# Seven products for a seventh pair of up projections, and GpSimd in place of VectorE for the weight sums

## The chip, the cores and the metric

The program runs on one core of one Trainium2 chip. The metric is the device time of one execution in microseconds; the kernel before has a median of 646.96 us over three runs (646.5 to 647.2). The profile is of one further execution, whose span from the first to the last instruction is 644.9 us; 2.1 us of the median lie outside that span. Engines are named as the profile names them: PE is TensorE, PEld its weight loads, DVE is VectorE, ACT is ScalarE, POOL is GpSimd, SP is SyncE, which issues most DMAs.

## The reference

One decoder layer on 512 tokens of width 1024: attention with a forget gate, a layer norm, a gated MLP with a causal convolution on the gate, a second layer norm, and a gated embedding that is added.

```python
def conv_ffn(x, w_up, conv_w, conv_b, w_down):
    u, g = jnp.split(x @ w_up, [FFN_DIM], axis=-1)
    g = causal_dwconv(g, conv_w, conv_b)
    return (jax.nn.gelu(g, approximate=False) * u) @ w_down
...
x = layer_norm(DEEPNORM_ALPHA * x + mix, ln_mix_g[i], ln_mix_b[i])
ffn = conv_ffn(x, ffn_w_up[i], ffn_conv_w[i], ffn_conv_b[i], ffn_w_down[i])
x = layer_norm(DEEPNORM_ALPHA * x + ffn, ln_ffn_g[i], ln_ffn_b[i])
```

FFN_DIM is 2816, that is 22 blocks of 128 columns, f = 0 to 21. Everything is float32.

## The kernel before, in words

**Products of split numbers.** A float32 product is made of three matmuls: each operand is cut into a high part (`whi`, made by ACT at L123) and the rest (`wlo`, made by DVE at L129 as raw minus high), and `three` (L147, the matmul is L152) adds high x high, high x low and low x high in PSUM.

**Units of weights.** The class `Weights` holds a list of units, up to 128x1024 numbers each, in the order in which PE uses them. SP loads a unit into one of four `raw` buffers (in the MLP every fifth unit goes into a fifth one, a part of the tile `side`). `cut_to` cuts units into `whi` and `wlo`, of which there are five pairs of buffers; in the MLP a unit is cut when PE is four units before it. A unit's cut thus frees the raw buffer for a load four or five units later. A unit may have a `make` function that first forms sums of weight blocks in place.

**Seven products in place of eight.** Some matrix products are done by halves with seven products of blocks in place of eight (a Strassen scheme). The weight side needs sums of blocks: `t12` forms two of them (L207, L208; the block that it subtracts is loaded into a slot of `side` at L204), `t3` one (L215), `t4` one (L222). Each sum is an operation of 128x512. For the down projection, the units of three pairs of blocks at a time (`down`, three parts) are made so. For the up projection, blocks are taken in pairs j = f // 2. Pairs in `UP_PAIRS` use seven products: `up_step` runs four steps for the gate g and for u in turn, three of 24 matmuls of 256 columns and one of 12. The other pairs use plain products of 24 matmuls of 512 columns, two for g and two for u. For pairs in `KEPT` the sums are made early, during attention, and kept in DRAM; the other pairs in `UP_PAIRS` make them with `t12`, `t3` and `t4`.

**Behind a pair.** With seven products the results are gathered in a tile E (L822 and L833 on DVE, L826, L827, L829 and L837 on ACT). After the last step the convolution (L759 on ACT, L760 and L762 on DVE), the GELU (L767, ACT) and the product with u (L768, DVE) run for both blocks at once. Then the operands of the down product are formed: four sums of E (L855 to L858, DVE) and their parts a, b and s (L863 on ACT, L864 on DVE). For a pair in `APART` the earlier pair's operands are formed only inside the first steps of this pair. There is one tile E.

**Order.** From f = 2 on, DVE and ACT keep the order in which the code is written. PE, POOL and SP are put in order by the framework. Units of the down product of the part before are put between the steps of the up product by `CHUNKS`. In pairs 1 and 2 (`DMA_PAIRS`) the low parts of plain units are formed by DMAs with accumulation on POOL's queue (L126); later POOL's queue carries accumulating DMAs that form the sums of the output gate's weights, each behind a small copy that waits for ACT (L279, L280, L281). The adders L659 and L661 add a finished down product to y.

```python
UP_PAIRS = (2, 3, 4, 6, 7, 9)
KEPT = (3, 4, 6, 7)
APART = (2, 3, 4, 7)
RAW_BUFS = 4
SPLIT_BUFS = 5
CHUNKS = (None, (1,) * 12, (1,) * 12, (2, 1) * 4)
```

Of the kernel before, what the change touches and what calls it, by code (L numbers as in the profile page):

```python
# [30 lines left out]

CHUNKS = (None, (1,) * 12, (1,) * 12, (2, 1) * 4)

UP_PAIRS = (2, 3, 4, 6, 7, 9)

KEPT = (3, 4, 6, 7)

DMA_PAIRS = (1, 2)

APART = (2, 3, 4, 7)  # L40
HALF = S // 2
ALPHA = 2.0 ** 0.25
EPS = 1e-5
# [20 lines left out]
class Weights:  # L64
# [40 lines left out]
    def cut_to(self, i):  # L105
        while self.cut < min(i, len(self.units)):
            self.load_to(self.cut + 1)

            self.make(self.cut)
            self.make(self.cut + 1)  # L110
            src, n, inner, make, home, by_dma = self.units[self.cut]
            t = self.raw.pop(self.cut)
            behind = ExitStack()
            if home is not None:
                hi, lo, first = home()
                behind.enter_context(self.tc.issue_after(first))
            else:
                hi, lo = [self.pool.tile([P, UNIT], F32R, tag=g, name=f"{g}{self.cut}", bufs=SPLIT_BUFS)
                          for g in ("whi", "wlo")]
            c = 0  # L120
            for piece in [t[:, :n]] if make is None else self.pieces.pop(self.cut):
                e = c + piece.shape[-1]
                self.nc.scalar.activation(hi[:, c:e], piece, AF.Copy)  # L123
                if by_dma:
                    self.nc.scalar.activation(lo[:, c:e], piece, AF.Copy, scale=-1.0)
                    self.nc.gpsimd.dma_start(lo[:, c:e].rearrange("p (a b) -> p a b", b=inner), src,  # L126
                                             accum_op=ALU.add)
                else:
                    self.nc.vector.tensor_sub(lo[:, c:e], piece, hi[:, c:e].bitcast(F32))  # L129
                c = e  # L130
            behind.close()
            self.parts[self.cut] = (hi, lo)
            self.cut += 1
# [9 lines left out]
def trunk_layer(ctx: ExitStack, tc: tile.TileContext, xT, x2d, pT, wqk, wv0, wv1, wv2, bf, wo, wup, cwb,  # L143
                wdn, wpl, wg, bg, gm, bm, gf, bff, out):
    nc = tc.nc
# [47 lines left out]
    def side(i):  # L193


        return aside[0][:, i, :]

    def t12(b11, i):
        def make(t):
            if t is None:  # L200
                to = side(i)
                if len(b11.shape) == 3:
                    to = to.rearrange("p (a b) -> p a b", b=P)
                nc.sync.dma_start(to, b11)  # L204
                return None
            t1, t2 = t[:, :512], side(i)
            nc.vector.tensor_sub(t1, t1, t2)  # L207
            nc.vector.tensor_sub(t2, t[:, 512:], t1)  # L208
            return [t1, t2]
        return make  # L210

    def t3(t):
        if t is None:
            return None
        nc.vector.tensor_sub(t[:, :512], t[:, 512:], t[:, :512])  # L215
        return [t]

    def t4(i):
        def make(t):
            if t is None:  # L220
                return None
            nc.vector.tensor_sub(t[:, :512], t[:, :512], side(i))  # L222
            return [t[:, :512]]
        return make

# [11 lines left out]
    def up_units(j):  # L237

        f0, f1 = 2 * j, 2 * j + 1
        if j in KEPT:  # L240
            return (lambda q: W.add(wup[f0, 1 - q], inner=P),
                    lambda q: W.add(kept[j, q][:, 0:4:3, :], inner=512),
                    lambda q: W.add([(kept[j, q][:, 2, :], 512), (wup[f1, 1 - q][:, 4:], 512)]),
                    lambda q: W.add(kept[j, q][:, 1, :], n=512))

        def unit(f, q, make=None, k0=0):
            return W.add(wup[f, 1 - q][:, k0:], n=(KD - k0) * P, inner=P, make=make,
                         by_dma=make is None and j in DMA_PAIRS)

        return (lambda q: unit(f0, q), lambda q: unit(f1, q, t12(wup[f0, 1 - q][:, :4], 3 + q)),  # L250
                lambda q: unit(f1, q, t3), lambda q: unit(f0, q, t4(3 + q), 4))
# [33 lines left out]
    for part in range(4):  # L285
# [3 lines left out]
        for i in range(2 * len(fs)):  # L289
            f, q = fs[i // 2], i % 2  # L290
            j, n = f // 2, i % 4
            if j in UP_PAIRS:
                stages = up_units(j)
# [4 lines left out]
            for _ in range(CHUNKS[part][i] if part else 0):  # L298
                if todo:
                    src, c, make = todo.pop(0)  # L300
                    u_dn[part - 1].append(W.add(src, n=c, inner=512, make=make))
            if j in UP_PAIRS and n == 3:
                for sq in range(2):
# [397 lines left out]
    def cut_tiles(kind, n, bufs, name, dtype=F32R, pool=spool):  # L701
        return [pool.tile([P, n, HALF], dtype, tag=f"{kind}{g}", name=f"{name}{g}", bufs=bufs) for g in "hl"]
# [89 lines left out]
    def up_step(j, st, s, E, amid=None):  # L792

        if st == 0:
            ups[j, s] = bank(f"{'gu'[s]}{2 * j}", "two" if j > 2 else None)
        ps = ups[j, s]
        z, x = ps[:, :HALF], ps[:, HALF:]
        hi, lo = W.get(u_up[j, st, s], 4)  # L800
        first, second = slice(0, HALF), slice(HALF, S)

        def go(to, col, on, a=None, sn=None, last=4):
            for k in range(4):
                w = slice((4 * col + k) * P, (4 * col + k + 1) * P)
                if a is None:
                    mh, ml = [v[:, 4 * sn + k, :] for v in xs]
                else:
                    mh, ml = [v[:, a[0] + k, a[1]] for v in (x1h, x1l)]
                three(to, hi[:, w], lo[:, w], mh, ml, k == 0 and not on, k == 3, on=on)  # L810

        e = E[:, (1 - s) * 2 * S:(2 - s) * 2 * S]
        c1 = side(7)[:, s * HALF:(s + 1) * HALF]
        if st == 0:
            go(z, 1, False, a=(4, first))
            go(x, 0, True, a=(0, first))
            nc.scalar.activation(c1, z, AF.Copy)
            nc.scalar.activation(z.rearrange("p (a b) -> p a b", b=P),
                                 zeros.unsqueeze(1).to_broadcast([P, 2, P]), AF.Copy)
            if amid is not None:  # L820
                amid()
            nc.vector.tensor_add(c1 if j in APART else e[:, :HALF], x, c1)  # L822
        elif st == 1:
            go(z, 0, True, sn=0)
            go(x, 1, True, sn=1)
            nc.scalar.activation(e[:, S:S + HALF], x, AF.Copy)  # L826
            nc.scalar.activation(e[:, S + HALF:], z, AF.Copy)  # L827
            if j in APART:
                nc.scalar.activation(e[:, :HALF], c1, AF.Copy)  # L829
        elif st == 2:  # L830
            go(z, 1, True, sn=3)
            go(x, 0, True, sn=2)
            nc.vector.tensor_add(e[:, S:], ps, e[:, S:])  # L833
        else:
            go(x, 0, True, a=(4, second))
            del ups[j, s]
            nc.scalar.activation(e[:, HALF:S], x, AF.Copy)  # L837
# [10 lines left out]
    def operand_sums(E):  # L848


        def e(n):
            return E[:, n * HALF:(n + 1) * HALF]

        a21, a11, a22, a12, s1, s2, s3, s4 = [e(n) for n in range(8)]
        nc.vector.tensor_add(s1, a21, a22)  # L855
        nc.vector.tensor_sub(s2, s1, a11)
        nc.vector.tensor_sub(s3, a11, a21)
        nc.vector.tensor_sub(s4, a12, s2)  # L858

    def operand_parts(ops, E):  # L860
        e3 = E.rearrange("p (a b) -> p a b", b=HALF)
        for (h, l), src in zip(ops, (e3[:, 1:4:2, :], e3[:, 2:3, :], e3[:, 4:, :])):
            nc.scalar.activation(h, src, AF.Copy)  # L863
            nc.vector.tensor_sub(l, src, h.bitcast(F32))  # L864
# [48 lines left out]
    for part in range(4):  # L913
# [3 lines left out]
        def between():  # L917
            for _ in range(next(slots, 0)):
                next(before)

        for f in range(6 * part, min(6 * part + 6, NF)):
# [3 lines left out]
            if f == 2:  # L925

                ordered.enter_context(tc.manual_schedule(
                    engines={mybir.EngineType.DVE, mybir.EngineType.Activation}))
            if q == 0 and j not in APART:
                E = hpool.tile([P, 8 * HALF], F32, tag="E", name=f"E{j}")  # L930
            if f == 0:
# [9 lines left out]
                continue  # L941
            if j in UP_PAIRS:
                if q == 0:
                    up_step(j, 0, 0, E)
                    between()
                    up_step(j, 0, 1, E, (lambda: operand_sums(E)) if j in APART else None)
                    if j in APART:
                        operand_parts(pending.pop(), E)
# [12 lines left out]
            else:  # L961
# [3 lines left out]
                n = 4 * (j - 3 * part) + 2 * q  # L965
# [10 lines left out]
            if q:  # L976
                if part < 3:
                    ops.append([cut_tiles("A", 2, 3, f"a{j}"), cut_tiles("B", 1, 5, f"b{j}", pool=hpool),
                                cut_tiles("S", 4, 4, f"s{j}")])
                    if j + 1 in APART:  # L980
                        pending.append(ops[-1])
# [3 lines left out]
                else:  # L985
# [4 lines left out]
                    ops.append((h, l))  # L990
            if j not in UP_PAIRS:
                between()
# [217 lines left out]
```

## Time and profile before

| | |
|---|---|
| Median of 3 runs | 646.96 us |
| Span of the profiled execution | 644.9 us |
| That execution with what lies outside the span, by the median | 2.1 us more |
| ACT | busy 384.7 us (60%) |
| POOL | busy 125.9 us (20%), 139 instructions |
| DMA, hardware queue of SP | 107.34 MB |

A row of the profile gives the line of the kernel, the engine, the operation, the tile written and the tiles read, the shape, and times. In a timeline the first two numbers are the start and the duration in microseconds; in brackets stands how long the engine was idle before, and for what. In the MLP, pair 0 begins at about 248 us, pair 1 at 271, pair 2 at 293, pairs 3, 4 and 5 at 313, 344 and 376, pairs 6, 7 and 8 at 404, 435 and 467, pairs 9 and 10 at 495 and 532; the last MLP product ends at 566 us.

### The profile page before, as it was taken

The page shows a single profiled execution, that of the slowest core. Times are in us where ns is not written, and L with a number is a line of the kernel's source. Part 1 is how long each engine was busy: PE and PEld are TensorE (multiplying, and loading weights), DVE is VectorE, ACT ScalarE, POOL GpSimd, SP SyncE. Part 2 cuts the span into 40 slices and gives each one's busy share as a digit, 9 for nine tenths or more (in the row PEclk, how much of TensorE's full clock was granted, in tenths as well). Part 3 has the DMA queues.
Part 4 walks back from the last instruction along what each step waited for, and adds up shares of the span by engine and source line. Part 5 has one row for each costly group of instructions (what it writes and reads, how often), then busy time and mean ns, then how long its engine had stood idle before and what let it go on. Part 6 is the DMA issues. An engine that isn't in the chain of part 4 may idle for free.

```text
span 644.9 us, 10078 instructions
## 1 busy us (share of the span) xinstructions
PE 638.9 (99%) x3630; PEld 563.4 (87%) x3630; DVE 533.5 (83%) x870; ACT 384.7 (60%) x685; POOL 125.9 (20%) x139
## 2 busy tenths in 40 slices
PE   8999999999999999999999999999999999999997
PEld 7899888888888889989999988999988998888886
DVE  6764779888888599857889987889897998689997
ACT  6653777877776317946656554647455455336872
POOL 0000544554456043110000010101011001002001
PEclk9999999999999999999999999999999999999999
DMA  8764524444578387684676849765746864681632
GB/s 284 250 236 127 210 85 153 172 177 159 205 256 314 127 261 220 140 219 137 209 219 170 216 132 243 196 212 149 235 130 207 189 219 113 159 283 57 232 113 98
DMA packets 49538, 121.08 MB, mean 188 GB/s; under 512 B 4881, under 2 KB 8721, under 8 KB 49489
## 3 DMA queue, kind: packets, MB, share of 16 engines
q1 hardware_dynamic: 44688, 107.34, 50.6%
q0 software_dynamic: 4800, 13.11, 11.0%
q8 instruction: 28, 0.46, 0.3%
q14 instruction: 22, 0.17, 0.1%
HBM read 107.72 MB, written 18.87 MB: 196 GB/s over the span
## 4 chain that ended last, share of the span: by engine, by line
PE 96%; DVE 2%; DMA 1%; SPq 0%; issue 0%; ACT 0%; DVEq 0%
PE g L152 18%; PE u L152 18%; PE pp L152 14%; PE x L152 8%; PE pl L152 7%; PE pv L152 7%; PE z L152 4%; PE r L152 3%; PE ap L152 3%; PE o L559 3%; PE t L546 2%; PE ao L152 2%; PE y L152 2%; PE s L509 2%; PE s L511 2%; PE p L152 1%
## 5 line engine op out<-in xcount | busy, mean ns | idle before, releaser
L123 ACT ACTIVATE whi<-raw 128x1024 fp32r<-128x1024 f32 (+5 forms) x137 | 128.3, 940 | 92.3 <-issue 12.5
L129 DVE TENSOR_TENSOR wlo<-raw,whi 128x1024 fp32r<-128x1024 f32 (+4 forms) x132 | 140.1, 1069 | 30.3 <-ACT whi L123 29.6
L533 POOL TENSOR_SCALAR pr<-pr,rl 128x128 f32<-128x128 f32 (+1 forms) x64 | 75.5, 1195 | 132.6 <-DVE rl L529 132.6
L280 POOL COPY neghalf<-neghalf 128x1 f32<-128x1 f32 x16 | 10.1, 633 | 246.1 <-ACT neghalf L279 246.1
L152 PE MATMUL g<-x1h,whi 128*128 128x256 f32 (+1 forms) x168 | 54.7, 326 | 0.0
L152 PE MATMUL g<-x1l,whi 128*128 128x256 f32 (+1 forms) x168 | 54.5, 324 | 0.0
L152 PE MATMUL g<-x1h,wlo 128*128 128x256 f32 (+1 forms) x168 | 54.5, 324 | 0.0
L152 PE MATMUL u<-x1l,whi 128*128 128x256 f32 (+1 forms) x160 | 53.0, 331 | 0.0
L152 PE MATMUL u<-x1h,wlo 128*128 128x256 f32 (+1 forms) x160 | 53.0, 331 | 0.0
L152 PE MATMUL u<-x1h,whi 128*128 128x256 f32 (+1 forms) x160 | 53.0, 331 | 0.0
L152 PE MATMUL pp<-xh,wlo 128*128 128x512 f32 x128 | 50.5, 394 | 0.0
L152 PE MATMUL pp<-xl,whi 128*128 128x512 f32 x128 | 50.0, 391 | 0.0
L152 PE MATMUL pp<-xh,whi 128*128 128x512 f32 x128 | 50.0, 391 | 0.0
L525 ACT ACTIVATE pr<-s,nm 128x128 f32<-128x128 f32 (+1 forms) x64 | 33.5, 527 | 9.1 <-DVE nm L521 8.9
L152 PEld LDWEIGHTS g<-x1h,whi 128*128 128x128 f32 x168 | 32.0, 190 | 3.4 <-issue 0.7
L152 PEld LDWEIGHTS g<-x1l,whi 128*128 128x128 f32 x168 | 32.0, 190 | 2.7
L152 PEld LDWEIGHTS g<-x1h,wlo 128*128 128x128 f32 x168 | 32.0, 190 | 2.5
L152 PEld LDWEIGHTS u<-x1h,whi 128*128 128x128 f32 x160 | 30.4, 190 | 3.0
L152 PEld LDWEIGHTS u<-x1l,whi 128*128 128x128 f32 x160 | 30.4, 190 | 2.9
L152 PEld LDWEIGHTS u<-x1h,wlo 128*128 128x128 f32 x160 | 30.4, 190 | 2.8
L123 ACT ACTIVATE whi<-side 128x512 fp32r<-128x512 f32 (+1 forms) x33 | 25.5, 783 | 10.3 <-PE u L152 3.6
L521 DVE CUSTOM_DVE_ANT_0 s<-s,mask 128x128 f32<-128x128 f32 (+1 forms) x64 | 30.0, 510 | 1.7 <-PE s L511 1.5
(635 smaller groups left out, 1869.9 us busy)
## 6 DMA issues: line engine op xcount, KB each, us to landing
raw<-wup SPq DMA_DIRECT2D x34, 512.0 KB, 5.9
raw<-wdn SPq DMA_DIRECT2D x23, 512.0 KB, 4.5
raw<-wqk SPq DMA_DIRECT2D x16, 512.0 KB, 3.3
ka<-wup SPq DMA_DIRECT2D x8, 512.0 KB, 4.2
kb<-wup SPq DMA_DIRECT2D x8, 512.0 KB
kept<-kb SPq DMA_DIRECT2D x8, 512.0 KB, 3.4
kept<-ka SPq DMA_DIRECT2D x8, 512.0 KB, 3.1
raw<-wo SPq DMA_DIRECT2D x8, 512.0 KB, 4.1
```

The costliest lines, as they stand in the source:

```text
L123: self.nc.scalar.activation(hi[:, c:e], piece, AF.Copy)
L129: self.nc.vector.tensor_sub(lo[:, c:e], piece, hi[:, c:e].bitcast(F32))
L152: nc.tensor.matmul(ps, lhsT, rhs, start=start and n == 0, stop=stop and n == 2, skip_group_check=on)
L280: with tc.issue_after(nc.gpsimd.tensor_copy(small[:, m + 32:m + 33], small[:, m:m + 1]).ins):
L509: nc.tensor.matmul(ps[:, :n], QA[:, q], KA[:, :n], start=True, stop=False)
L511: nc.tensor.matmul(ps[:, :n], qb[0:68, q], kb[0:68, :n], start=False, stop=True)
L521: last_mask[:] = [nc.vector.tensor_tensor_reduce(ps[:, :w], ps[:, :w], mask[:, S - w:], -1.0, BIG, op0=ALU.add, op1=ALU.min, accum_out=nm[ ...
L525: nc.scalar.activation(pr[:, off:off + w], ps[:, :w], AF.Exp, bias=nm[:, i:i + 1], scale=-1.0, accum_out=ls[:, i:i + 1])
L533: nc.gpsimd.tensor_scalar_mul(pr[:, off:off + w], pr[:, off:off + w], rl[:, i:i + 1])
L546: nc.tensor.transpose(ps[:, w:w + P], pr[:, o:o + P], ident)
L559: nc.tensor.matmul(ps[:, q0:], V[:, j, h], p[:, o:o + w], start=j == 0 and n == 0, stop=j == NT - 1 and n == 1)
```

## The change

Pair 8 (blocks 16 and 17) joins `UP_PAIRS` and `APART`, so that its up products are seven products of halves; it is not in `KEPT`, so its weight sums are made by `t12`, `t3` and `t4`. All sums of these three functions go from DVE to POOL. `cut_to` calls `make` for the unit that is cut and for the two behind it, where it was for one behind it.

```diff
-UP_PAIRS = (2, 3, 4, 6, 7, 9)
+UP_PAIRS = (2, 3, 4, 6, 7, 8, 9)
...
-APART = (2, 3, 4, 7)
+APART = (2, 3, 4, 7, 8)
...
-            self.make(self.cut)
-            self.make(self.cut + 1)
+            for n in range(3):
+                self.make(self.cut + n)
...
-            nc.vector.tensor_sub(t1, t1, t2)
-            nc.vector.tensor_sub(t2, t[:, 512:], t1)
+            nc.gpsimd.tensor_sub(t1, t1, t2)
+            nc.gpsimd.tensor_sub(t2, t[:, 512:], t1)
...
-        nc.vector.tensor_sub(t[:, :512], t[:, 512:], t[:, :512])
+        nc.gpsimd.tensor_sub(t[:, :512], t[:, 512:], t[:, :512])
...
-            nc.vector.tensor_sub(t[:, :512], t[:, :512], side(i))
+            nc.gpsimd.tensor_sub(t[:, :512], t[:, :512], side(i))
```

The order shows how instructions move. Numbers behind raw, whi and wlo are units; pair 8 takes the units 109 to 116 with plain products (down units among them) and 109 to 120 with seven, so that every later unit's number rises by four. On POOL, at the end of pair 7 and in pair 8, the difference between the two kernels is this (+ is new; L280 and L281 are the gate's DMAs):

```order
 L281 DMA gt4_74<-gt2_72 128x512
+L215 TENSOR_TENSOR raw110_4876<-raw110_4876 128x512
+L222 TENSOR_TENSOR raw112_4957<-raw112_4957,side_2707 128x512
+L207 TENSOR_TENSOR side_2707<-side_2707 128x512
+L208 TENSOR_TENSOR side_2707<-side_2707 128x512
+L207 TENSOR_TENSOR raw114_4991<-raw114_4991,side_2707 128x512
+L208 TENSOR_TENSOR side_2707<-raw114_4991 128x512
+L222 TENSOR_TENSOR raw115_5012<-raw115_5012,side_2707 128x512
+L215 TENSOR_TENSOR raw116_5033<-raw116_5033 128x512
+L215 TENSOR_TENSOR raw117_5111<-raw117_5111 128x512
 L280 COPY neghalf_96<-neghalf_96 128x1
```

Between two of the gate's DMAs there now stand nine sums in a row; the L207 and L208 of unit 113 (in `side`) and of 114 belong to pair 8's second step. In all POOL has 60 sums, the 52 that DVE had and 8 for pair 8.

On DVE, behind the last step of pair 7 (its blocks are 14 and 15, its tile E7), before the change:

```order
L768 TENSOR_TENSOR E7_4811<-a14_5046,E7_4811 128x512
L855 TENSOR_TENSOR E7_4811<-E7_4811 128x256
L856 TENSOR_TENSOR E7_4811<-E7_4811 128x256
L857 TENSOR_TENSOR E7_4811<-E7_4811 128x256
L858 TENSOR_TENSOR E7_4811<-E7_4811 128x256
L864 TENSOR_TENSOR a7l_5055<-E7_4811,a7h_5054 128x512
L864 TENSOR_TENSOR b7l_5057<-E7_4811,b7h_5056 128x256
L864 TENSOR_TENSOR s7l_5059<-E7_4811,s7h_5058 128x1024
L222 TENSOR_TENSOR raw114_4989<-raw114_4989,side_2707 128x512
L129 TENSOR_TENSOR wlo113_5077<-side_2707,whi113_5076 128x1024
```

With the change, the same operations of pair 7 stand later, and pair 8's stand among them. Between the last L768 and the first row here lie the cuts of units 113 and 114, an L822 and four additions to y:

```order
L129 TENSOR_TENSOR wlo115_5133<-raw115_5012,whi115_5132 128x512
L855 TENSOR_TENSOR E7_4811<-E7_4811 128x256
L856 TENSOR_TENSOR E7_4811<-E7_4811 128x256
L857 TENSOR_TENSOR E7_4811<-E7_4811 128x256
L858 TENSOR_TENSOR E7_4811<-E7_4811 128x256
L822 TENSOR_TENSOR side_2707<-u16_5130,side_2707 128x256
L864 TENSOR_TENSOR a7l_5061<-E7_4811,a7h_5060 128x512
L864 TENSOR_TENSOR b7l_5063<-E7_4811,b7h_5062 128x256
L864 TENSOR_TENSOR s7l_5065<-E7_4811,s7h_5064 128x1024
L129 TENSOR_TENSOR wlo116_5178<-raw116_5033,whi116_5177 128x1024
```

The cut of unit 116, whose products are the third step of pair 8's gate, now stands behind the whole of pair 7's operands.

On DVE, behind the last step of pair 8, with the change (unit 125 is the third down unit of the last part, 126 is pair 9's second step):

```order
L768 TENSOR_TENSOR E8_5175<-a16_5393,E8_5175 128x512
L855 TENSOR_TENSOR E8_5175<-E8_5175 128x256
L856 TENSOR_TENSOR E8_5175<-E8_5175 128x256
L857 TENSOR_TENSOR E8_5175<-E8_5175 128x256
L858 TENSOR_TENSOR E8_5175<-E8_5175 128x256
L864 TENSOR_TENSOR a8l_5402<-E8_5175,a8h_5401 128x512
L864 TENSOR_TENSOR b8l_5404<-E8_5175,b8h_5403 128x256
L864 TENSOR_TENSOR s8l_5406<-E8_5175,s8h_5405 128x1024
L129 TENSOR_TENSOR wlo125_5425<-raw125_5306,whi125_5424 128x1024
L822 TENSOR_TENSOR E9_5420<-g18_5421,side_2707 128x256
```

Before the change only one L768 stood between pair 8's last matmul and L855, since the plain products had let block 16, and block 17's convolution, go ahead; now the convolutions and products of both blocks stand there, and the cut of unit 125 behind them.

## The prediction

> **What bounds the kernel now.** I read the page's first part, then the chain that ended last, then what TensorE waited for, then the two stretches that the change rebuilds.
>
> ```profile
> span 644.9 us, 10078 instructions
> PE 638.9 (99%) x3630; PEld 563.4 (87%) x3630; DVE 533.5 (83%) x870; ACT 384.7 (60%) x685; POOL 125.9 (20%) x139
> PE 96%; DVE 2%; DMA 1%; SPq 0%; issue 0%; ACT 0%; DVEq 0%
> ```
>
> TensorE (PE) is busy for 99% of the span and carries 96% of the chain, so only fewer matmul cycles or a wait avoided can make this kernel faster. The list of PE's own waits holds two rows, both near the start:
>
> ```profile
> PE warm L333 <- DVE zeros L329: 1.1, 1, 1.1
> PE pv L152 <- ACT whi L123: 0.9, 2, 0.7
> ```
>
> In the whole MLP, from 247 to 566 us, PE waits for nothing. VectorE (DVE) and GpSimd (POOL) matter there only if they become late. The two stretches below are pair 8 and pair 9 (columns: window, sum, then PE, PEld, DVE, ACT, POOL busy, clock, DMA share, GB/s):
>
> ```profile
> 466.63:495.46 28.83, 28.83 (x128) 23.59 (x128) 23.27 (x35) 14.35 (x22) 3.02 (x4) 1.00 0.64 178
> 495.46:532.01 36.55, 36.55 (x242) 33.67 (x241) 35.95 (x55) 20.16 (x34) 2.22 (x4) 1.00 0.69 193
> ```
>
> DVE is at 23.27 of 28.83 us in pair 8, but at 35.95 of 36.55 in pair 9, which already has seven products and whose sums DVE makes. So DVE is near its limit there and PE still does not wait. The granted clock is 1.00 in both.
>
> **The matmuls.** From the chain, in order of time (start, us):
>
> ```profile
> 463.75 1.43 PE g L152 x12
> ...
> 474.81 5.44 PE u L152 x24
> ...
> 495.46 2.87 PE g L152 x24
> ...
> 556.52 2.72 PE x L152 x12
> ```
>
> Pair 8 now is four groups of 24 matmuls 512 wide, 4 x 5.44 = 21.8 us. With seven products it is six groups of 24 at 256 wide and two of 12, 6 x 2.87 + 2 x 1.43 = 20.1 us. The sum's first term is **-1.6 us**, and it is the only gain, since nothing else lies on PE's path. A down unit between them takes 2.72 us, or half of that, 1.36, for the units of one block.
>
> **What leaves and joins DVE.** 52 sums leave it in the MLP; rows of the window 247 to 570:
>
> ```profile
> L129 DVE TENSOR_TENSOR wlo<-raw,whi 128x1024 fp32r<-128x1024 f32 x55 | 66.8, 1221 | 4.5 <-ACT whi L123 4.4
> L661 DVE TENSOR_TENSOR y<-y,x 128x512 f32<-128x512 f32 x18 | 11.5, 681 | 0.0
> L222 DVE TENSOR_TENSOR raw<-raw,side 128x512 f32<-128x512 f32 x12 | 8.2, 684 | 0.0
> L207 DVE TENSOR_TENSOR raw<-raw,side 128x512 f32<-128x512 f32 x8 | 5.5, 686 | 2.6 <-DMA raw<-wdn 2.6
> ```
>
> Each is 0.68 to 0.69 us long, as are the additions to y. Two DVE operations overlap by some 0.08 us, as the starts of two cuts show, which are 1.14 us apart while one takes 1.22:
>
> ```profile
> 490.51 1.22 DVE L129 TENSOR_TENSOR wlo<-side,whi 128x1024 fp32r<-128x1024 f32 x1
> 491.65 1.22 DVE L129 TENSOR_TENSOR wlo<-raw,whi 128x1024 fp32r<-128x1024 f32 x1
> ```
>
> So a cut of 1024 holds DVE for 1.14 us, an operation of 512 for 0.60, of 256 for 0.36, and the 52 sums free 31 us of it. No PE wait goes with them: **0**. Pair 8's own work grows: four cuts of 1024 (4.6 us) become four of 1024 and six of 512 (8.2), and four additions out of PSUM join (1.9), together 5.5 us more, in a stretch that PE leaves 1.6 us sooner. Its eight new sums are POOL's.
>
> The place that decides is the handover from pair 7 to pair 8. Pair 7 ends on PE at 466.63. What follows it on DVE now (timeline):
>
> ```profile
> 467.78 0.75 DVE L760 SCALAR_TENSOR_TENSOR a<-E,cw,a 128x511 f32<-128x511 f32 x1 [0.93 <-ACT a L759]
> 472.25 0.43 DVE L855 TENSOR_TENSOR E<-E 128x256 f32<-128x256 f32 x1
> 473.72 0.69 DVE L864 TENSOR_TENSOR a7l<-E,a7h 128x512 fp32r<-128x512 f32 x1
> 474.94 1.23 DVE L864 TENSOR_TENSOR s7l<-E,s7h 128x1024 fp32r<-128x1024 f32 x1 [0.19 <-ACT s7h L863]
> ```
>
> The convolutions and products of pair 7 hold DVE until 472.25, 5.6 us behind PE. By the new order there then stand, up to the cut of unit 116 (pair 8's third group): cuts 113 and 114 (4 x 0.60), two L822 (0.7), four additions to y (2.4), cut 115 (0.6), L855 to L858 (1.4), three L864 (2.1) with the 0.2 us that s7l waits for ACT, cut 116 (1.14), 11.0 us in all. Cut 116 is done 16.6 us behind pair 7's end. PE needs it after 2.87 + 2.72 + 2.87 + 1.36 + 2.87 + 1.36 + 2.87 = 16.9 us. The **slack is 0.3 us**, with DVE not pausing once. In the kernel before, PE spends 5.44 us on each of these groups and needs no such cut so soon.
>
> The second such place is new too: pair 8 ends as pair 7 did, and pair 9 follows it at once with the down product of unit 125, whose cut stands behind pair 8's last L864. By the rows above s7l ends 9.5 us behind its pair (474.94 + 1.23 - 466.63); the next cut ends 1.14 later, at 10.7. PE comes to unit 125 after 2.87 + 2 x 2.72 + 2.87 = 11.2 us. Slack **0.5 us**.
>
> **What POOL's sums cost DVE.** No run here has a sum on POOL. The nearest are its multiplications L533, beside which DVE makes sums of two SBUF tiles (L456 to L458, L129):
>
> ```profile
> 149.78 0.92 POOL L533 TENSOR_SCALAR pr<-pr,rl 128x256 f32<-128x256 f32 x1
> 178.30 0.95 POOL L533 TENSOR_SCALAR pr<-pr,rl 128x128 f32<-128x128 f32 x1 [6.40 <-DVE rl L529]
> 197.70 2.17 POOL L533 TENSOR_SCALAR pr<-pr,rl 128x256 f32<-128x256 f32 x1
> L533 POOL TENSOR_SCALAR pr<-pr,rl 128x512 f32<-128x512 f32 x16 | 25.5, 1594 | 0.0
> ```
>
> ```profile
> 178.13 0.66 DVE L456 TENSOR_TENSOR kb<-kb 128x512 f32<-128x512 f32 x1
> 178.82 0.74 DVE L457 TENSOR_TENSOR kb<-kb,ka 128x512 f32<-128x512 f32 x1
> ...
> 180.14 0.68 DVE L458 TENSOR_TENSOR ka<-ka,kb 128x512 f32<-128x512 f32 x1
> ```
>
> ```profile
> 197.94 1.21 DVE L129 TENSOR_TENSOR wlo<-raw,whi 128x1024 fp32r<-128x1024 f32 x1
> 199.08 0.88 DVE L458 TENSOR_TENSOR ka<-ka,kb 128x512 f32<-128x512 f32 x1
> ```
>
> The two engines stand in each other's way. POOL's 256 columns take 0.92 us alone and 2.17 beside the cut at 197.94: it waited the cut out, 1.25 us. Behind it L458 takes 0.88 instead of 0.68, so DVE paid 0.20; behind POOL's 128 columns L457 takes 0.74, some 0.06 over the usual. Each 128 columns more cost DVE 0.14 us more. A sum reads two inputs of 512, 1024 columns in all: by that line 0.06 + 7 x 0.14 = 1.0 us; if only 512 count, 0.5; if it finds DVE idle or reading PSUM, 0. The bounds are **0 and 1.0 us of DVE for each sum**; nothing excludes the lower one, and a gain is excluded, since the sum's own time on DVE is counted above. I take 0.5, the value for a read of this width, and about what 1.0 gives where every second DVE operation behind a sum is spared.
>
> How many sums fall into the two chains: a buffer's load is issued when the cut four or five units before it is done, lands 4.5 to 5.9 us later, and its sum follows.
>
> ```profile
> raw<-wup SPq DMA_DIRECT2D x34, 512.0 KB, 5.9
> raw<-wdn SPq DMA_DIRECT2D x23, 512.0 KB, 4.5
> ```
>
> Cuts 109 to 112 stand just ahead of pair 7's convolutions, so the loads of 114 to 117 land from about that pair's end on, and the sums of 114 (the second), 115, 116, 117 and one of 118 to 120 run beside the first chain: 5. Beside the second run those of 127 and 128, two each: 4. The stalls are 5 x 0.5 - 0.3 = **2.2 us** and 4 x 0.5 - 0.5 = **1.5 us**. Elsewhere the MLP's sums meet a DVE that their leaving has freed: 0.
>
> The Trainium skill (SBUF — State Buffer, Who interferes with whom) says that a DVE operation with two SBUF inputs and a GpSimd operation that reads SBUF lock each other out, and that the one that starts first holds the port for its whole instruction. POOL's wait of 1.25 us agrees; DVE's 0.20 us behind an operation of 0.92 does not look like a whole instruction. What that rule would make of the time is rival D.
>
> **Loads and POOL's queue.** Pair 8's loads grow from 2 to 4 MB. At 178 GB/s over 28.83 us the stretch moves 5.1 MB now, at a DMA share of 0.64; 7.1 MB at that cost is a share of some 0.95 over 27 us. I cost it at 0, hidden by the units loaded ahead; without that cover a load late by a microsecond is late on PE by as much. Calling `make` for a third unit loads nothing sooner that the ring of buffers holds back, but it puts the sums ahead of L126's and L281's DMAs in POOL's queue; those serve units and gate products that PE reaches several groups later: 0.
>
> **The sum.** -1.6 + 2.2 + 1.5 = +2.1 us. The profiled execution has a span of 644.9 us, and the runs a median of 646.96, 2.1 more for what lies outside the span; I put the change on the median: **649.1 us**.
>
> **Rivals.**
> B, the sums hide. They fall where DVE waits (0.93 us before L760) or reads PSUM, and both slacks hold: -1.6, 645.3 us. For it: DVE loses 31 us of work and pair 9 does without a PE wait at 98% now. Against it: the slacks are 0.3 and 0.5 us. **0.28**.
> C, half of it. At 0.2 us for a sum, what L458 paid, the stalls are 0.7 and 0.3, and 646.4 us remains, not to be told from no change. **0.22**.
> A, the forecast, from 0.45 us for each sum (9 x 0.45 - 0.8 - 1.6 = +1.7, 648.7 us) to 1.0 (4.7 + 3.5 - 1.6 = +6.6, 653.6 us); 648.7 to 653.6 is its own range. **0.40**.
> D, a port held for the whole instruction: with 1.59 us for each sum, as L533 takes at 512 columns, 9 x 1.59 - 0.8 - 1.6 = +11.9, 658.9 us. The 0.20 us speaks against it. **0.04**.
> E, POOL itself is late. Units 126 to 129 need two sums each; at 1.59 us and a wait of 0.6 a unit takes 4.4 us, against PE's 2.8, and over four units loses 6.4 us, of which a head start of one unit's sums, 4.4 us, covers most: 2.0 us on top of the forecast, 651.1 us. **0.06**.
> That the change does not do what it says is excluded by the order: all 60 sums stand on POOL and pair 8 has its seven products.
>
> **How the numbers follow.** A measurement of this kernel tells about 0.2%, 1.3 us, from no change. Slower by more than that are A, D and E, 0.50; within it is C, 0.22; faster is B, 0.28. The range goes from B with the spread of the runs, 645.0, up to 0.9 us for each sum (9 x 0.9 - 0.8 - 1.6 = +5.7), 652.7. Of A it leaves out the top, and D.
>
> **What would show it.** Right: PE waits behind DVE's wlo or ACT's E for unit 116 and unit 125, cuts and L855 to L864 in pairs 8 and 9 longer than now (0.43, 0.69, 1.22 us), POOL's sums well over 1.6 us there. Wrong: no PE wait in pair 8 and a DVE with pauses there (then B), waits of ACT for POOL's raw or side (then E), or a sum on POOL far from 1.6 us.

## The result, and the profile after

The changed kernel takes 670.51 us, the median of four runs (669.54 to 671.66), against 646.73 us (646.33 to 647.2) for the kernel before on the same chip: a ratio of 1.0372, with a 95% interval of 1.0360 to 1.0384. It is **slower by 3.7%**. The direction was forecast, the size was not: 649.1 us and a range up to 652.7.

The page of the changed kernel has these lines where the kernel before had 99% and 533.5 us for PE and DVE and 96% of the chain on PE:

```profile
span 667.8 us, 10374 instructions
PE 644.0 (96%) x3702; PEld 569.4 (85%) x3702; DVE 555.1 (83%) x828; ACT 390.1 (58%) x703; POOL 223.9 (34%) x199
PE 76%; DVE 13%; DMA 4%; issue 3%; ACT 2%; POOL 1%; SPq 0%; DVEq 0%; POOLq 0%; ACTq 0%
```

Read the DVE number first. DVE has 42 instructions fewer than before (828 against 870), since the sums have left it, and it is busy for 21.6 us **longer**. So a busy row on DVE also holds time in which DVE is held up.

Where the time went is read from windows that begin at the same matmuls in both kernels: the MLP up to the second u step of pair 4, from there to pair 8, pair 8, pair 9 and the first units of pair 10, and the rest. Columns: window, its length, then PE, PEld, DVE, ACT and POOL busy (x instructions), PE's granted clock, DMA share, GB/s. Before:

```profile
247.00:358.40 111.40, 111.40 (x760) 103.79 (x759) 92.78 (x136) 74.12 (x117) 10.63 (x13) 1.00 0.70 187
358.40:466.60 108.20, 108.20 (x681) 98.09 (x680) 92.23 (x127) 59.91 (x101) 10.56 (x14) 1.00 0.70 199
466.60:495.50 28.90, 28.90 (x129) 23.66 (x128) 23.34 (x35) 14.39 (x23) 3.02 (x4) 1.00 0.64 178
495.50:548.20 52.70, 52.70 (x313) 47.01 (x311) 49.59 (x72) 28.72 (x48) 4.12 (x6) 1.00 0.61 168
548.20:644.90 96.70, 92.79 (x441) 77.26 (x439) 83.03 (x114) 51.81 (x74) 10.44 (x12) 1.00 0.49 157
```

After, the same stretches:

```profile
247.00:360.00 113.00, 111.03 (x755) 103.18 (x753) 92.16 (x118) 72.24 (x115) 37.50 (x29) 1.00 0.67 185
360.00:471.40 111.40, 109.89 (x678) 99.44 (x679) 94.22 (x113) 61.29 (x102) 32.70 (x30) 0.98 0.67 190
471.40:508.40 37.00, 30.24 (x201) 27.66 (x199) 32.13 (x36) 17.78 (x35) 19.01 (x13) 0.91 0.55 168
508.40:571.10 62.70, 54.98 (x312) 48.20 (x313) 58.57 (x59) 30.63 (x52) 35.03 (x25) 0.95 0.52 147
571.10:667.80 96.70, 92.80 (x441) 77.20 (x439) 84.86 (x116) 51.77 (x75) 12.50 (x13) 1.00 0.51 165
```

The lengths differ by +1.6, +3.2, +8.1, +10.0 and 0.0 us, together the 22.9 us by which the spans differ. So pair 8 and what follows it hold most of the loss, but 4.8 us arise earlier, in pairs that the change of `UP_PAIRS` does not touch. In the first four windows PE is idle for 18.0 us (324.1 us of length against 306.1 busy), and it is busy for 306.1 us where 301.2 - 1.6 = 299.6 were due. These 6.5 us more lie in windows with a granted clock of 0.98, 0.91 and 0.95.

PE's longest waits in the MLP (for whom, total, times, longest):

```profile
PE x L152 <- ACT whi L123: 7.6, 1, 7.6
PE g L152 <- DVE side L822: 4.4, 1, 4.4
PE u L152 <- DVE side L822: 2.0, 1, 2.0
```

The 7.6 us are at unit 125, the place that the prediction named for its second stall. The 4.4 us are in pair 8's second gate step, unit 113, one gate step earlier than the place that it named for the first; L822 stands there behind the cut of unit 113. The wait of 2.0 us falls in pair 4, where no stall was forecast.

What DVE does ahead of unit 125 shows the mechanism. DVE behind pair 8 with the change (start, duration):

```profile
511.53 1.78 DVE L760 SCALAR_TENSOR_TENSOR a<-E,cw,a 128x511 f32<-128x511 f32 x1
513.34 1.66 DVE L762 SCALAR_TENSOR_TENSOR a<-E,cw,a 128x510 f32<-128x510 f32 x1
514.92 1.78 DVE L760 SCALAR_TENSOR_TENSOR a<-E,cw,a 128x511 f32<-128x511 f32 x1
516.74 1.66 DVE L762 SCALAR_TENSOR_TENSOR a<-E,cw,a 128x510 f32<-128x510 f32 x1
518.32 3.44 DVE L768 TENSOR_TENSOR E<-a,E 128x512 f32<-128x512 f32 x2
521.80 1.37 DVE L855 TENSOR_TENSOR E<-E 128x256 f32<-128x256 f32 x1
523.20 1.37 DVE L856 TENSOR_TENSOR E<-E 128x256 f32<-128x256 f32 x1
524.49 0.41 DVE L857 TENSOR_TENSOR E<-E 128x256 f32<-128x256 f32 x1
```

And POOL at the same time, the first three and the last of eight sums:

```profile
510.84 1.91 POOL L207 TENSOR_TENSOR raw<-raw,side 128x512 f32<-128x512 f32 x1 [12.13 <-DMA raw<-wup]
512.84 1.62 POOL L208 TENSOR_TENSOR side<-raw 128x512 f32<-128x512 f32 x1
514.41 1.75 POOL L207 TENSOR_TENSOR raw<-raw,side 128x512 f32<-128x512 f32 x1
...
522.97 1.32 POOL L208 TENSOR_TENSOR side<-raw 128x512 f32<-128x512 f32 x1
```

The two engines **take turns**, one operation of DVE for one of POOL (eight DVE operations are lengthened, beside eight sums), until POOL's queue is empty at 524.29; at 524.49 DVE's operation of 256 columns is back at 0.41 us. POOL's queue held eight sums: the first of them had waited 12.13 us for its load, and the others stood behind it.

The Trainium skill (SBUF — State Buffer, Who interferes with whom) says that a DVE instruction with two SBUF inputs contends with a GpSimd instruction that reads SBUF. These rows agree: beside each sum the DVE row is 0.9 to 1.0 us longer (L760 1.78 us against the 0.75 quoted of before, L855 1.37 against 0.43).

### The profile page after: what moved, and what is told of

It is laid out like the page before. It is cut to its first block, busy times and chain, and to the rows that moved or that the text cites. A ratio compares the mean times of both kernels' runs of the same rounds, so it can differ in the third digit from the quotient of the medians.

```text
span 667.8 us, 10374 instructions
## 1 busy us (share of the span) xinstructions
PE 644.0 (96%) x3702; PEld 569.4 (85%) x3702; DVE 555.1 (83%) x828; ACT 390.1 (58%) x703; POOL 223.9 (34%) x199
## 4 chain that ended last, share of the span: by engine, by line
PE 76%; DVE 13%; DMA 4%; issue 3%; ACT 2%; POOL 1%; SPq 0%; DVEq 0%; POOLq 0%; ACTq 0%
PE pp L152 13%; PE u L152 12%; PE g L152 11%; PE pl L152 6%; PE pv L152 6%; PE x L152 4%; DVE wlo L129 4%; PE r L152 3%; PE ap L152 3%; PE ao L152 3%; PE o L559 3%; PE t L546 3%; PE z L152 2%; DVE a L760 2%; DVE a L762 2%
## 5 line engine op out<-in xcount | busy, mean ns | idle before, releaser
L129 DVE TENSOR_TENSOR wlo<-raw,whi 128x1024 fp32r<-128x1024 f32 (+4 forms) x135 | 160.0, 1200 | 39.5 <-ACT whi L123 38.7
L152 PE MATMUL g<-x1h,whi 128*128 128x256 f32 (+1 forms) x164 | 51.8, 316 | 2.8 <-ACT E L837 1.9
L152 PE MATMUL g<-x1l,whi 128*128 128x256 f32 (+1 forms) x164 | 51.5, 314 | 0.0
L152 PE MATMUL g<-x1h,wlo 128*128 128x256 f32 (+1 forms) x164 | 51.5, 314 | 0.0
L152 PE MATMUL u<-x1h,whi 128*128 128x256 f32 (+1 forms) x156 | 50.1, 321 | 0.1
L129 DVE TENSOR_TENSOR wlo<-side,whi 128x512 fp32r<-128x512 f32 (+1 forms) x35 | 36.4, 1056 | 5.3 <-ACT whi L123 5.0
L152 PE MATMUL g<-xsh,whi 128*128 128x256 f32 x112 | 32.2, 288 | 4.4 <-DVE side L822 4.4
L152 PE MATMUL u<-xsh,whi 128*128 128x256 f32 x112 | 32.5, 290 | 2.0 <-DVE side L822 2.0
L215 POOL TENSOR_TENSOR raw<-raw 128x512 f32<-128x512 f32 x13 | 20.1, 1545 | 40.0 <-DMA raw<-wdn 10.8
L767 ACT ACTIVATE a<-a 128x512 f32<-128x512 f32 x22 | 13.9, 631 | 32.8 <-DVE a L762 32.8
```

What stands on the lines that cost most here:

```text
L152: nc.tensor.matmul(ps, lhsT, rhs, start=start and n == 0, stop=stop and n == 2, skip_group_check=on)
L215: nc.gpsimd.tensor_sub(t[:, :512], t[:, 512:], t[:, :512])
L767: nc.scalar.activation(a, a, AF.Gelu)
```

## The experiments

Theory P: POOL's sums stop DVE's operations on two SBUF tiles, for the length of a sum at each turn, and this makes the cuts and E late. Rivals: H, pair 8's handovers are tight whoever makes the sums; L, POOL delivers its sums late for ACT's cuts; Q, it is the distance of three units. All ratios are to the kernel before on the same chip.

**1. Pair 8 alone**, sums on DVE, two units ahead.

```diff
-UP_PAIRS = (2, 3, 4, 6, 7, 9)
+UP_PAIRS = (2, 3, 4, 6, 7, 8, 9)
...
-APART = (2, 3, 4, 7)
+APART = (2, 3, 4, 7, 8)
```

> Pair 8 with seven products, all sums on VectorE (DVE), two units ahead as before; nothing on GpSimd (POOL). Theory P (POOL's sums stop DVE): no POOL sum, so nearly all of the change's +23.8 us goes; -1.6 us of matmuls stay, and pair 8's handovers, tight even before, may keep some stall, since eight sums more (8 x 0.60 us) lie on DVE: 645 to 650 us. Theory H (pair 8's own handover, whoever makes the sums): pair 8 stays near 37 us on PE and the time is above 655 us.

651.48 us, ratio 1.0086 (1.0071 to 1.0101). This lies between: a fifth of the loss is there without POOL. PE's waits in the MLP are four of 1.1 to 1.5 us, all in pairs 8 and 9, so H is true of that fifth, and P's range is missed by 1.5 us.

**2. Sums on POOL, pair 8 plain**, three units ahead.

```diff
-UP_PAIRS = (2, 3, 4, 6, 7, 8, 9)
+UP_PAIRS = (2, 3, 4, 6, 7, 9)
...
-APART = (2, 3, 4, 7, 8)
+APART = (2, 3, 4, 7)
```

> All 52 sums of before on POOL, three units ahead; pair 8 plain. Theory P: the stalls of the other pairs remain (about 5 us before pair 8 and one of 5 to 8 us in pair 9, where seven-product bursts meet the operands of the pair before): 655 to 664 us. Theory H: without pair 8 nothing is tight, 645 to 648 us.

657.15 us, ratio 1.0170 (1.0154 to 1.0185). P holds. The two parts alone cost 5.2 and 10.9 us, together 16.1, and 23.8 in one kernel. That would fit two parts that each take the cover that the other needed; no run shows it.

**3. The changed kernel with sums on DVE**, still three units ahead (`nc.gpsimd.tensor_sub` back to `nc.vector.tensor_sub` in `t12`, `t3`, `t4`).

> The changed kernel with its sums back on DVE, still three units ahead. Theory P: within 2 us of the kernel with pair 8 on DVE and two units ahead; a little slower if DVE, which runs in order, now waits for a load one unit further ahead. Theory Q (the distance ahead, which moves the sums past POOL's DMAs and asks for loads earlier): it keeps a large part of the loss, over 655 us.

656.87 us, ratio 1.0172 (1.0155 to 1.0189), 5.4 us above experiment 1: Q's number. The list of DVE's waits between 460 and 535 us has a row that experiment 1 does not have:

```profile
DVE raw L215 <- DMA raw<-wdn: 4.4, 1, 4.4
```

DVE keeps the written order, so a sum that is called a unit earlier stands waiting for its load, and all DVE work waits behind it. On POOL the same wait stops only POOL, so this price need not be part of the changed kernel's loss; experiment 7 tries that directly.

**4. Sums on DVE and idle sums on POOL.** Experiment 3 with, beside each sum, a subtraction on POOL whose result nobody reads.

```diff
+            for _ in range(2):
+                nc.gpsimd.tensor_sub(spare[0], t[:, 512:], t[:, 512:])
             nc.vector.tensor_sub(t1, t1, t2)
             nc.vector.tensor_sub(t2, t[:, 512:], t1)
...
```

> As the kernel with three units ahead and sums on DVE, and beside each of the 60 sums POOL makes a subtraction of 128x512 of two SBUF inputs into a tile that nobody reads, when the same block has landed. Nobody waits for POOL's result. Theory P (contention between the two engines): DVE's operations on two SBUF inputs lengthen by 1.0 to 1.1 us for each of POOL's that falls beside them, and the time is 10 us or more above the kernel without them, above 660 us. Theory L (POOL's sums are late for ScalarE's cuts): within 2 us of the kernel without them.

687.32 us, ratio 1.0644 (1.0615 to 1.0673), 30.5 us above experiment 3. No wait in this trace's MLP, of an engine or of SP's loads, names one of these subtractions, so contention alone can cost as much as the change did, and more.

**5. No sums at all.** The changed kernel without its 60 sums.

```diff
-            nc.gpsimd.tensor_sub(t1, t1, t2)
-            nc.gpsimd.tensor_sub(t2, t[:, 512:], t1)
             return [t1, t2]
...
```

> The changed kernel with all 60 sums of weight blocks left out on both engines (the products are then of other numbers; their count and shapes stay). By the prediction's working the two handovers have slacks of 0.3 and 0.5 us without sums, so PE waits for nothing and -1.6 us remains: 644 to 645.5 us against a kernel before of 646.3 to 647. If the handovers of pair 8 were mis-sized (theory H), PE still waits at units 113, 116 and 125 and the time is above 647 us.

646.63 us, ratio 1.0008 (0.9998 to 1.0017), between the two expectations. The -1.6 us is not there, even with sums that cost nothing. PE's two waits in the MLP are these:

```profile
PE u L152 <- DVE E L829: 0.9, 1, 0.9
PE x L152 <- DVE wlo L129: 0.6, 1, 0.6
```

The second is unit 125; the first is pair 8's last u step, which waits for the addition that is L833 in the changed kernel. Between 480 and 500 us the waits of DVE and ACT name what that addition stood behind, a cut that waited for a load:

```profile
DVE wlo L129 <- ACT whi L123: 4.5, 2, 3.9
ACT whi L123 <- DMA raw<-wup: 4.4, 1, 4.4
```

The same DVE operations as behind pair 8 above, here without POOL:

```profile
497.26 0.74 DVE L756 SCALAR_TENSOR_TENSOR a<-E,cw,a 128x511 f32<-128x511 f32 x1
...
502.53 0.42 DVE L853 TENSOR_TENSOR E<-E 128x256 f32<-128x256 f32 x1
```

(L756 is L760 there, L853 is L857.) From the first convolution to the third sum of E are 5.27 us here and 12.96 us (524.49 - 511.53) in the changed kernel. Eight POOL sums thus cost 7.7 us, **0.96 us each**.

**6. Idle sums alone.** Experiment 5 with 60 subtractions on POOL into a bf16 tile that nobody reads, and **7. two units ahead** in place of three, sums on POOL:

```diff
-            nc.gpsimd.tensor_sub(t1, t1, t2)
-            nc.gpsimd.tensor_sub(t2, t[:, 512:], t1)
+            for _ in range(2):
+                nc.gpsimd.tensor_sub(spare[0], t[:, 512:], t[:, 512:])
...
```

```diff
-            for n in range(3):
+            for n in range(2):
                 self.make(self.cut + n)
```

> As the kernel without sums, but POOL makes 60 subtractions of 128x512 of two SBUF inputs, of the same blocks when they have landed, into a tile that nobody reads. Theory P (DVE and POOL exclude each other): about the time of the changed kernel, 665 to 671 us, though nobody waits for POOL. Theory L (lateness of POOL's sums for the cuts): the time of the kernel without sums, within 2 us.

> The changed kernel with make called two units ahead, as before, in place of three; sums on POOL. Theory P: the same sums stop the same DVE work at nearly the same times, 665 to 676 us. Theory Q (three units ahead moves sums into the handovers; two ahead would let them pass): below 662 us. Theory L: POOL's sums come later for ScalarE's cuts, above 672 us with ACT's waits for raw and side on the chain.

Experiment 6 gives 661.11 us, ratio 1.0225 (1.0210 to 1.0241): 14.5 us above no sums, so L falls as the main cause, but 9 us below the changed kernel, so P as written falls short too. Experiment 7 gives 672.24 us, ratio 1.0395 (1.0358 to 1.0431), within 2 us of the change: Q falls for sums on POOL. The time lies in P's range and, barely, in L's, so it does not decide between these two.

**8. Idle sums in the form of the real ones.** The 9 us that were left could be lateness, or the form of the idle sums. Here 45 of the 60 read two different blocks and write f32; the 15 of `t3` read two different halves and still write bf16.

```diff
-                nc.gpsimd.tensor_sub(spare[0], t[:, 512:], t[:, 512:])
+                nc.gpsimd.tensor_sub(t[:, 512:], t[:, 512:], t[:, :512])
...
```

> As the kernel with idle subtractions, but 45 of the 60 write 512 f32 columns of the block's own unused half and read two different halves, as the real sums do (those of t3 keep the bf16 tile that nobody reads). It asks why the changed kernel is 9 us above the idle subtractions. Theory P1 (the price of a real sum on DVE is higher, 1.0 us against the 0.77 us of an idle one, and the stalls follow it): 665 to 670 us. Theory L (the rest is the wait of ScalarE's cuts for sums that POOL's queue delivers late): within 1.5 us of the idle subtractions, 659.5 to 662.5 us.

670.06 us, ratio 1.0359 (1.0342 to 1.0376): the changed kernel's time, though no engine waits for a sum in its MLP. The form of the subtraction made the 9 us. A POOL group of experiment 6 and one of this (mean ns behind the busy time):

```profile
L208 POOL TENSOR_TENSOR spare<-raw 128x512 bf16<-128x512 f32 x20 | 27.2, 1359 | 43.7 <-DMA raw<-wdn 26.5 <-DMA raw<-wup 16.3
```

```profile
L208 POOL TENSOR_TENSOR raw<-raw 128x512 f32<-128x512 f32 x20 | 32.6, 1634 | 44.2 <-DMA raw<-wup 16.7 <-DMA raw<-wdn 11.8 <-issue 9.6
```

The second block that is read makes the difference, not the f32 that is written. Among the subtractions with nothing beside them, one of `t3` here, which writes bf16, takes 1.29 us (at 282.45 us), one that writes f32 takes 1.30 (at 290.05), and one of experiment 6, which reads one half twice, takes 1.04 (at 281.11).

**9. POOL busy without reading.** Experiment 5 with, for each sum, a copy of one column and three memsets on POOL.

```diff
+            for _ in range(2):
+                nc.gpsimd.tensor_copy(spare[0][:, :1], t[:, 512:513])
+                for _ in range(3):
+                    nc.gpsimd.memset(spare[0], 0.0)
...
```

> As the kernel with idle subtractions, but each of them is a copy of one column and three memsets of 128x512 bf16, which read nothing from SBUF, together about as long. If it is POOL's reading of two SBUF inputs that stops DVE (theory P as the trace suggests), the time is within 2 us of the kernel without sums. If any work of POOL on SBUF stops DVE, it comes out near the kernel with idle subtractions.

650.27 us, ratio 1.0063 (1.0044 to 1.0082), 1.6 us outside the first expectation and far from the second. POOL is busy for 241.7 us, more than in the changed kernel, yet DVE's operations are as long as with no POOL work, and DVE is busy for 507.9 us, as in experiment 5 (508.3). The groups of the large cut and of L760 in the MLP, in this kernel (where that line is L769):

```profile
L129 DVE TENSOR_TENSOR wlo<-raw,whi 128x1024 fp32r<-128x1024 f32 x56 | 67.6, 1221 | 14.6 <-ACT whi L123 14.2
L769 DVE SCALAR_TENSOR_TENSOR a<-E,cw,a 128x511 f32<-128x511 f32 x14 | 10.5, 747 | 2.5 <-ACT a L768 2.5
```

And in the changed kernel:

```profile
L129 DVE TENSOR_TENSOR wlo<-raw,whi 128x1024 fp32r<-128x1024 f32 x55 | 79.9, 1465 | 15.0 <-ACT whi L123 14.6
L760 DVE SCALAR_TENSOR_TENSOR a<-E,cw,a 128x511 f32<-128x511 f32 x14 | 15.5, 1104 | 0.9 <-ACT a L759 0.9
```

An operation of DVE with one input in PSUM pays nothing either. At 268 us in the changed kernel two DVE operations follow each other, each beside a sum of POOL. L857 reads E twice from SBUF; L762 reads g from PSUM:

```profile
267.93 1.32 DVE L857 TENSOR_TENSOR E<-E 128x256 f32<-128x256 f32 x1
269.16 0.73 DVE L762 SCALAR_TENSOR_TENSOR a<-g,cw,a 128x510 f32<-128x510 f32 x1
```

```profile
267.66 1.29 POOL L207 TENSOR_TENSOR raw<-raw,side 128x512 f32<-128x512 f32 x1 [3.66 <-DMA raw<-wup]
269.03 1.37 POOL L208 TENSOR_TENSOR side<-raw 128x512 f32<-128x512 f32 x1
```

L857 takes 1.32 us, 0.90 over its 0.42; L762, inside L208 from end to end, takes 0.73, and 0.75 in the kernel before. So POOL's reads and DVE's second SBUF input collide, not POOL's activity as such.

The 3.6 us above experiment 5 are not DVE's; the chain of waits passes there through a load into `side` of 8.37 us. The idle sums and these copies leave one delay of the real sums in place: a load into a buffer waits until POOL is done with the buffer. SP's loads wait 48.4 us in all for POOL here, 31.0 in experiment 6, 37.5 in experiment 8 and 31.1 in the changed kernel. With more of that waiting than they have, this kernel loses 3.6 us against experiment 5, where those two lose 14.5 and 23.4, so that delay is not what costs them most.

**10 and 11. More cover from down units.** Experiment 1, with one down unit (10) or two (11) moved from the end of pair 7 into pair 8, and pair 9's third one moved two steps later.

```diff
-CHUNKS = (None, (1,) * 12, (1,) * 12, (2, 1) * 4)
+CHUNKS = (None, (1,) * 12, (1,) * 7 + (0, 2) + (1,) * 3, (1, 1, 2, 2, 2, 1, 2, 1))
...
+CHUNKS = (None, (1,) * 12, (1,) * 6 + (0, 0, 2, 2, 1, 1), (1, 1, 2, 2, 2, 1, 2, 1))
```

> Pair 8 with seven products and sums on DVE, two units ahead, and the down units stand elsewhere: one that stood before the last step of pair 7 stands behind the first step of pair 8, and the third one of pair 9 (the first that reads pair 8's operands) two steps later. Theory H (what is left of the loss on DVE are the two handovers, 3.5 us in pair 8 and 3.6 us in pair 9): PE gets 2.7 us more cover in pair 8 and 5.7 us more in pair 9, and most of the loss goes: 645 to 648 us. Rival (DVE is simply full over pairs 8 and 9, so the wait moves to the next cut): 649.5 to 652 us.

> As the kernel with moved down units, but two down units are moved from the end of pair 7 into pair 8, so its steps have 5.4 us more cover. Theory H: as the one with one unit moved or up to 1 us faster, 644.5 to 647 us; if pair 7's own last steps now lack cover, a new stall of 1 to 3 us there. Rival (DVE full): 649.5 to 652 us.

655.38 and 653.56 us, ratios 1.0136 (1.0121 to 1.0151) and 1.0120 (1.0099 to 1.0141), slower than experiment 1: both theories missed. The order of cuts on ACT and DVE moves with the units. In 11 the unit with pair 8's operands is now cut behind the sums of the unit ahead of it, as its chain of waits shows (start, duration; the cut is the ACT row):

```profile
508.59 0.70 DVE raw L207
509.31 0.70 DVE side L208
...
510.57 1.05 ACT whi L123
...
511.66 0.50 PE x L152
```

No version here beats the kernel before, and experiment 5 says why it is hard: with sums for nothing there would be nothing to gain in this order of work.

**12. Sums in halves.** Each POOL sum as two of 256 columns.

```diff
-        nc.gpsimd.tensor_sub(t[:, :512], t[:, 512:], t[:, :512])
+        for c in (0, 256):
+            nc.gpsimd.tensor_sub(t[:, c:c + 256], t[:, c + 512:c + 768], t[:, c:c + 256])
...
```

> The changed kernel with each of POOL's 60 sums made as two of 256 columns. In the changed kernel the two engines take turns, one operation of POOL for each operation of DVE, and DVE pays 1.0 us at each turn. Theory W (the wait is for POOL's whole operation, whatever its length): each DVE operation beside a burst pays about 0.5 to 0.7 us, a burst lasts twice as many turns, and the chains of some twelve operations behind pairs 7 and 8 pay a little less than now: 663 to 670 us. Theory F (a turn costs DVE a fixed 1.0 us however short POOL's operation is): twice as many turns at the same price, above 672 us.

672.53 us, ratio 1.0404 (1.0387 to 1.0422). By its time this fits F, by its rows W. DVE behind pair 8 (L763 is L760, L858 is L855):

```profile
514.43 1.23 DVE L763 SCALAR_TENSOR_TENSOR a<-E,cw,a 128x511 f32<-128x511 f32 x1
...
521.42 0.85 DVE L858 TENSOR_TENSOR E<-E 128x256 f32<-128x256 f32 x1
...
528.47 1.74 DVE L129 TENSOR_TENSOR wlo<-raw,whi 128x1024 fp32r<-128x1024 f32 x1
```

The convolution takes 1.23 us, 0.48 over its 0.75: half the price at each turn. The burst reaches to the cut of unit 125 at 528.47, so that 14 DVE operations are lengthened where eight were. From the first convolution to the end of that cut the chain lasts 15.8 us, against 17.2 in the changed kernel and 9.5 in experiment 5, a little less, as W says. W's range for the whole kernel is missed because other waits of PE grew: the one in pair 4 is 3.9 us against 2.0, and pair 8 has four of 1.4 to 2.2 us where there were 4.4, 1.9 and 0.4. Why they grew was not followed.

## Why the prediction was wrong in size

**What bounds the kernel.** Right: PE sets the end, and the loss came as waits of PE behind DVE's L822 and for ACT's cut at unit 125.

**-1.6 us of matmuls.** Right in kind, too large by half a microsecond: in experiment 5 PE is busy for 637.9 us against 638.9 before, and between the first matmuls of pairs 8 and 9 it takes 28.5 us, 0.9 of them a wait, where it took 28.8. This gain of 1.0 to 1.2 us was given back by the two stalls of 0.9 and 0.6 us.

**The price of a sum, 0 to 1.0 us, taken as 0.5.** This is the step that failed first. The line through L457 and L458 gave 1.0 at 1024 columns read, and the measured price is 0.96. The choice of 0.5 rested on a read of 512 columns, or on every second DVE operation being spared. In the chains none is spared: while POOL's queue holds a sum that is ready, POOL takes each second turn. Nor was the 0.20 us of L458 cheap for its 256 columns: the same line gives 0.48 at the 512 columns that a half sum reads, and experiment 12 measured 0.48. With 1.0 in place of 0.5 the prediction's own sum still ends at 653.6 us, the top of rival A; the rest of the miss is in the terms that follow.

**The number of sums, 5 and 4.** Too low. Behind pair 7 the cut of unit 116 is done 24.3 us after the pair's end on PE, against 16.7 in experiment 5, and POOL makes eight sums beside that chain (a ninth starts only during the cut of unit 116); behind pair 8 there are eight too. A chain that is slowed lasts longer and meets more sums, and a load that is late lets sums gather. The first eight cost 7.6 us (0.95 each) and the second 7.7, where 2.5 and 2.0 stood.

**The slacks, 0.3 and 0.5 us.** The first chain was worked out well: 16.6 us against the 16.7 of experiment 5. The second was wrong by a little over a microsecond: two cuts stand between pair 8's end and its first convolution, which starts 2.7 us behind PE there, not the 1.15 us read from pair 7, and unit 125 waits 0.6 us without any sum.

**Loads at 0.** Off by the 0.9 us that pair 8's last step waits in experiment 5.

**Elsewhere 0, since DVE is freed.** Wrong: 4.8 us are lost up to pair 8. In part this is the same price (L857 at 357.71 us takes 1.49 us ahead of pair 4's wait), but the chain to that wait also passes through a sum that ACT's cut waits for, 1.91 us on POOL (at 352.74) where DVE took 0.68. How the 4.8 us divide was not separated. DVE is busy for 508.3 us with no sums (experiment 5), 543.7 with 60 sums on it (experiment 1), 555.1 with 60 sums on POOL. A sum costs DVE 0.59 us when DVE makes it and 0.78 us, averaged over all 60, when POOL does. So in the balance the sums' leaving freed nothing.

**What the sum left out.** PE's waits cost more than their length. The windows around the wait at unit 125 in the changed kernel:

```profile
519.70:527.30 7.60, 0.14 (x2) 0.00 (x0) 7.35 (x9) 2.96 (x6) 5.33 (x4) 0.79 0.00 0
527.30:529.80 2.50, 2.24 (x5) 1.34 (x6) 2.50 (x5) 2.47 (x7) 1.10 (x2) 0.50 0.37 21
529.80:532.30 2.50, 2.50 (x11) 2.06 (x10) 2.50 (x5) 2.47 (x6) 0.00 (x0) 0.78 0.88 85
532.30:534.80 2.50, 2.50 (x23) 2.50 (x22) 2.50 (x6) 0.76 (x3) 0.00 (x0) 1.00 0.84 198
```

After 7.6 us without matmuls the granted clock is 0.50, then 0.78, and 1.00 only in the window that begins 5 us after PE went on. Such stretches lie behind the 6.5 us that PE is busy beyond its due. The Trainium skill (TensorE: Matmul & The Clock Gate, Part 1: The HAM clock gate) tells of a half-rate clock after an idle window of about 3.4 us, and full rate after a busy one; the rows agree. PE's 18.0 us without work and those 6.5, less the 1.6 of matmuls, are the 22.9 us by which the span grew.

**The rivals.** B (the sums hide) was never to be had: even without sums the kernel only equals the one before. C took for each sum the 0.20 us that L458 paid beside a quarter of the columns. D was nearest in kind, every sum paid for at each turn, at a chance of 0.04, but priced a sum at 1.59 us where 0.96 was measured; its 658.9 us is still too low, since it kept nine sums, both slacks and nothing elsewhere. E (POOL late) falls as the main cause by experiment 8, which is as slow though no engine waits for a sum; pair 4 shows one place where POOL is late.

## What to carry to other kernels

Work on two SBUF tiles is not taken off DVE by giving it to POOL while DVE itself runs operations on two SBUF tiles: here each sum cost DVE more from POOL's side than on DVE. Count the price of a contention that no run has shown yet at its upper bound when the other engine's queue will hold several such operations, and count them all, since they gather behind a late load. Before costing a gain, take the disputed work out altogether: if the kernel is then no faster than before, the rest need not be priced.

## What the runs showed of the hardware

- In the bursts DVE and POOL alternated, one operation each, and DVE's price per turn followed the length of POOL's operation: 0.96 us at 512 columns (a sum with nothing beside it took 1.29 us), about 0.48 at 256.
- POOL's memsets, 0.53 us each and 180 in the MLP, cost DVE's operations nothing (1221 and 747 ns, as in the kernel without sums).
- A DVE operation with one input in PSUM paid nothing beside a sum (L762, 0.73 us), where one with both inputs in SBUF paid 0.90 just before.
- Subtractions on POOL that read one half twice cost the kernel 14.5 us over 60 of them, those that read two different blocks 23.4 us.
